# One root for all rows, ScalarE rounding for the recurrent gates, one PSUM pool through the up projection, and a new order of early weight loads, in a one-core decoder layer

## The chip, the cores and the metric

The kernel runs on one core of a Trainium2 chip. The metric is the device time of one execution in microseconds (us). All times below are counted from the start of the profiled span. TensorE is written PE in the profile, VectorE DVE, ScalarE ACT, GpSimd POOL and SyncE SP. SP and POOL issue DMAs here: SP plain ones, POOL those that add to what stands at the destination.

## What is computed

One layer on a sequence of 1024 rows of width 1024, in float32:

```
mod = c @ ada_w + ada_b                                  # six vectors: shift, scale, gate, twice
h   = rmsnorm(x) * g1 * (1 + sc1) + sh1
xr, yr, q, k, v, ga, gb = split(h @ w_in)                # seven "comps" of 1024 columns, numbered 0 to 6
xr  = causal_dwconv(xr)                                  # 4 taps
y_a = rg_lru(xr) * gelu(yr)                              # gates: sigmoid(xr @ wa), sigmoid(xr @ wx), per head of 128
y_b = stick_breaking_attention(rms(q), rms(k), v)        # 8 heads of 128
x   = x + gt1 * ((sigmoid(ga) * y_a + sigmoid(gb) * y_b) @ w_out)
h2  = rmsnorm(x) * g2 * (1 + sc2) + sh2
up  = causal_dwconv(h2 @ ffn_up)                         # 3 taps, 6144 columns: 24 pairs of gate and value blocks
out = x + gt2 * ((gelu(gate) * value) @ ffn_down)
```

## The kernel before

Every float32 product is made of three matmuls on rounded operands: each operand is split into a high part (rounded to fp32r) and a low part (the rest), and high times high, high times low and low times high are added up in PSUM. So each weight tile and each activation tile costs one cast (mostly ACT) and one subtraction (mostly DVE, `lo_of`).

**Opening** (about 0 to 76 us). Its order is written out by hand (`tc.manual_schedule()`), each engine's queue follows the program text. Eight tiles `xr` hold 128 rows of x each. `squares(t)` sums their squares on ACT, `norm(hf, on_act)` makes the reciprocal root (`rsqrt`, twelve small DVE instructions) for four rows at a time and scales these rows, some on ACT, the others on DVE. A unit n is a pair (j, hf): block j of 128 channels and half hf of the sequence. `channels(n)` transposes four 128x128 pieces on TensorE and lets ACT write the high part and a float32 copy, with shift and scale; `rest(n)` makes the low part on DVE. `scale_shift(j)` computes shift and scale of block j on DVE from two loaded tiles (`load_modulation`), each a dot product with the broadcast c. While units appear, three products of the first head are accumulated block by block: comps 3, 2 and 6 (`FIRST`). Their weights come with `first_load` and are split by `first_split` (cast on ACT, subtraction on POOL). The loop at the end of the opening runs over the sixteen units; turn n prepares unit n + 2 and multiplies unit n.

**Heads** (to 605 us): projections, attention and gate b of eight heads, in an order that a planner chooses from priorities and modelled costs.

**Recurrent stage** (605 to 865 us), planned too: for each head `lru_head` convolves on DVE and ACT, rounds the result `xc` to `xh` on POOL, subtracts `xl` on DVE and multiplies both with the gates' weights (L578 to L580); the activations follow on ACT, with changes of its table.

**Output projection** (to 945 us): `out_block(t)` for eight row blocks, accumulators `ao` from `acc_tile`, three buffers of two PSUM banks; evacuation on DVE (`og`). Half of the second normalization and of the up weights of steps 0 and 1 is prepared in between.

**Up projection** (945 to 1416 us), again by hand. It uses seven block products a step (Strassen's scheme on halves of channels and of the sequence), for 24 steps f. The sums of weight blocks are made by DMAs: a load on SP (`load`), then an accumulating DMA on POOL (`add`), and between the adds ACT and DVE split what stands there (`x1`, `x2_`, `x3`, `x4`). Six steps begin early (`early(f, n)`, twelve products on the first half of the sequence), interleaved by the slots `s_` of a list `plan` with `second_half(i)`, which normalizes the second half and reloads the first half from DRAM (`b11`, `b21` from `h2d`), and with `keep`, which splits the normalized sums. Each step needs accumulators bx and by (and bz where it didn't begin early), taken from `bank_tile`: after the output projection the PSUM pool is closed and a new pool `ups` gives six buffers of one bank.

**Down projection** (1416 us to the end): 24 blocks in four groups, its own PSUM pool.

## Time and profile before

| | |
|---|---|
| time, median of 3 runs | 1684.32 us (1684.28 to 1685.02) |
| the profiled execution's own time | 1682.83 us |
| its span in the profile | 1681.1 us |
| PE busy | 1634.8 us, 97% of the span |
| DVE, ACT, POOL busy | 1073.5, 798.4 and 219.9 us |
| bytes moved by DMA | 197.74 MB, mean 118 GB/s |

The span runs from the first to the last instruction of the core; the time of an execution is longer by what lies around it, here 1.7 us. A busy share is an average over all stages; what a stage waits for is in its own rows. The granted TensorE clock reads 1.00 in every stretch of the table of stages. Idle time of an engine counts only where TensorE, or whatever ends last, waits for it.

### The profile page before, as it was taken

The numbers are of one execution on the slowest core, as the hardware profiler recorded it, in microseconds if no ns is written. First come the engines' busy times: TensorE is split into PE (matmuls) and PEld (weight loads), VectorE is DVE, ScalarE is ACT, GpSimd is POOL, SyncE is SP. The second block draws the span as 40 slices with busy tenths as digits, with TensorE's granted clock in tenths as the row PEclk, the third lists the DMA queues.
The fourth block names the chain that finished last, engine by engine and source line by source line (L and its number), as shares of the span: only waits on it lengthen the run. The fifth ranks groups of instructions, "written<-read, shape, count | busy, mean of one in ns | idle before, by whom it ended". The sixth has DMA issues, their size and how long they took to land.

```text
span 1681.1 us, 22203 instructions
## 1 busy us (share of the span) xinstructions
PE 1634.8 (97%) x8170; PEld 1368.2 (81%) x8170; DVE 1073.5 (64%) x1739; ACT 798.4 (47%) x1338; POOL 219.9 (13%) x366
## 2 busy tenths in 40 slices
PE   3999999999999999989999999999999999999999
PEld 1898898898898887878888767888888887888887
DVE  6776857957857735856666568866666657425372
ACT  5645544644635526766464544444455445423100
POOL 2011111110100101310100122111111110001110
PEclk9999999999999999999999999999999999999999
DMA  8222322222222232221133597665566656514232
GB/s 316 88 76 78 99 76 76 85 86 82 76 86 85 76 125 70 72 79 57 44 124 145 203 229 184 150 147 134 128 140 143 147 119 201 175 63 151 67 121 100
DMA packets 94796, 197.74 MB, mean 118 GB/s; under 512 B 10128, under 2 KB 19552, under 8 KB 94688
## 3 DMA queue, kind: packets, MB, share of 16 engines
q1 hardware_dynamic: 80288, 170.11, 30.3%
q0 software_dynamic: 14400, 26.22, 9.5%
q8 instruction: 64, 1.05, 0.3%
q14 instruction: 44, 0.36, 0.1%
HBM read 164.79 MB, written 30.45 MB: 116 GB/s over the span
## 4 chain that ended last, share of the span: by engine, by line
PE 85%; DMA 4%; ACT 4%; DVE 4%; issue 2%; POOL 1%; SPq 0%; ACTq 0%; POOLq 0%; DVEq 0%
PE acc L150 27%; PE ad L1063 16%; PE bx L817 12%; PE by L817 6%; PE accv L393 6%; PE ao L662 5%; PE py L459 3%; PE bz L817 3%; PE tp L446 2%; DMA R<-in_ffn_up_dram 1%; DMA Q<-in_ffn_up_dram 1%; PE z L421 1%; PE z L422 1%; PE z L420 1%; ACT L550 1%
## 5 line engine op out<-in xcount | busy, mean ns | idle before, releaser
L769 POOL DMA_DIRECT2D R<-in_ffn_up_dram x72 | 63.4, 923 | 195.7 <-DVE ul L60 138.8
L1077 DVE TENSOR_TENSOR sum<-ad,sum 128x1024 f32<-128x1024 f32 (+1 forms) x26 | 29.4, 1140 | 85.6 <-PE ad L1063 84.0
L430 POOL TENSOR_SCALAR_AFFINE_SELECT stk<-stk 128x128 f32<-128x128 f32 x64 | 23.4, 366 | 409.0 <-ACT stk L425 392.0
L909 ACT COPY yv<-bx 128x512 f32<-128x512 f32 x36 | 21.2, 589 | 115.8 <-PE bx L817 115.8
L425 ACT ACTIVATE stk<-z,rkq 128x128 f32<-128x128 f32 (+3 forms) x96 | 57.2, 596 | 37.9 <-PE z L422 27.9
L574 POOL TENSOR_SCALAR xh<-xc 128x512 fp32r<-128x512 f32 x16 | 40.2, 2510 | 220.3 <-DVE xc L568 148.3
L60 DVE TENSOR_TENSOR ul<-Q,uh 128x512 fp32r<-128x512 f32 x42 | 28.9, 688 | 61.7 <-ACT uh L717 61.7
L60 DVE TENSOR_TENSOR ul<-R,uh 128x512 fp32r<-128x512 f32 x72 | 47.9, 687 | 31.2 <-ACT uh L717 31.2
L717 ACT CAST uh<-R 128x512 fp32r<-128x512 f32 x72 | 42.7, 618 | 51.8 <-DMA R<-in_ffn_up_dram 51.4
L438 DVE TENSOR_TENSOR_SCAN stk<-stk 128x128 f32<-128x128 f32 (+1 forms) x64 | 53.8, 841 | 15.5 <-POOL stk L434 9.9
L843 DVE SCALAR_TENSOR_TENSOR c<-yg,par,c 128x1023 f32<-128x1023 f32 (+1 forms) x48 | 61.5, 1280 | 2.8 <-ACT c L841 2.2
L843 DVE SCALAR_TENSOR_TENSOR c<-yv,par,c 128x1023 f32<-128x1023 f32 (+1 forms) x48 | 61.2, 1276 | 0.0
L135 DVE SCALAR_TENSOR_TENSOR ada<-ada,cb 128x1024 f32<-128x1024 f32 x48 | 60.4, 1271 | 0.0
L442 DVE TENSOR_TENSOR beta<-beta,stk 128x128 f32<-128x128 f32 (+3 forms) x96 | 54.0, 562 | 7.9
L60 DVE TENSOR_TENSOR al<-tp,ah 128x128 fp32r<-128x128 f32 (+3 forms) x96 | 51.7, 549 | 10.9 <-ACT ah L448 10.7
L448 ACT CAST ah<-tp 128x128 fp32r<-128x128 f32 (+3 forms) x96 | 45.4, 489 | 27.2 <-PE tp L446 19.1
L426 ACT ACTIVATE beta<-z,rkq 128x128 f32<-128x128 f32 (+3 forms) x96 | 57.0, 594 | 0.0
L446 PE MATMUL tp<-ident,beta 128*128 128x128 f32 x288 | 46.1, 274 | 0.0
L459 PE MATMUL py<-al,vh 128*128 128x256 f32 (+1 forms) x160 | 45.5, 284 | 0.0
L150 PE MATMUL acc<-hh,w_0h 128*128 128x512 f32 x96 | 37.6, 419 | 7.6 <-ACT w_0h L190 4.8
L459 PE MATMUL py<-ah,vl 128*128 128x256 f32 (+1 forms) x160 | 44.9, 281 | 0.0
L459 PE MATMUL py<-ah,vh 128*128 128x256 f32 (+1 forms) x160 | 44.2, 276 | 0.0
(522 smaller groups left out, 5496.4 us busy)
## 6 DMA issues: line engine op xcount, KB each, us to landing
ada<-in_ada_t_dram SPq DMA_DIRECT2D x48, 512.0 KB, 3.3
R<-in_ffn_up_dram POOLq DMA_DIRECT2D x72, 256.0 KB, 5.5
td<-c SPq DMA_DIRECT2D x24, 512.0 KB, 4.0
dn<-td SPq DMA_DIRECT2D x48, 256.0 KB, 7.0
dn<-in_ffn_down_dram SPq DMA_DIRECT2D x48, 256.0 KB, 3.4
R<-in_ffn_up_dram SPq DMA_DIRECT2D x24, 256.0 KB, 4.5
Q<-in_ffn_up_dram SPq DMA_DIRECT2D x24, 256.0 KB, 6.1
Q<-in_ffn_up_dram POOLq DMA_DIRECT2D x24, 256.0 KB, 4.0
```

Of the source, the lines that this page charges most:

```text
L60: return tt(out=out_, in0=full, in1=hi_.bitcast(F32), op=ALU.subtract)
L135: stt(out=t, in0=t, scalar=1.0, in1=cb, op0=ALU.mult, op1=ALU.mult, accum_out=mod[:, n:n + 1])
L150: mm(acc[hf], w[:, k % 4], r[k][hf], start=(k == 0 and i == 0), stop=(k == NB - 1 and i == 2))
L393: mm(acc[:, t * 2 * P:(t + 1) * 2 * P], r[k][hf][:, ts_], w[:, k % 2], start=(k == 0 and i == 0 and t == 0), stop=(k == NB - 1 and i == 2 ...
L425: act(st[:, :n], z[:, :n], AF.Sigmoid, scale=rkq[:, 16 + qb:17 + qb])
L446: nc.tensor.transpose(tp[:, t * P:(t + 1) * P], beta[:, t * P:(t + 1) * P], ident)
L459: mm(py[:, e0 * P:2 * P], vv[:, kb, d0:d0 + P], aa[kb // 4][:, kb % 4, e0:2], start=(kb == 0 and i == 0), stop=(kb == nkb - 1 and i == 2))
L662: mm(halves(acc, nf), m[k][hf][:, ts_], w[nf], start=(k == 0 and i == 0), stop=(k == NB - 1 and i == 2))
L769: nc.gpsimd.dma_start(blk(raw[f, key]), piece(f, row, half), accum_op=ALU.add)
L817: mm(bank, w[a][:, ks], Bm[n][b][k], start=(first and k == 0 and i == 0), stop=(last and k == 3 and i == 2), skip_group_check=True)
L843: stt(out=cs[f, i][:, d:], in0=y[:, :S - d], scalar=col("fw", (2 - d) * 48 + j), in1=cs[f, i][:, d:], op0=ALU.mult, op1=ALU.add)
L1063: mm(halves(acc, nf), dparts[f, hf][a][:, ts_], dparts[f, 2 + nf][w], start=(first and i == 0), stop=(last and i == 2))
```

## The change

Four edits, all in `trunk`.

1. Opening: the DMA queue begins with c and the modulation of block 0, then all eight rows of x, then the weights of comps 3 and 2, the modulation of block 1, the weights of comp 6 and the other modulations. One root is taken over all eight rows; two of the rows (3 and 4) are scaled on ACT, six on DVE. The subtraction for the low weights of the three first comps moves from POOL to DVE (`first_rest`). The first units' products are reordered: comp 3 of block 0 for both halves ahead of the loop, comps 2 and 6 of block 0 in the loop's first two turns.
2. Recurrent stage: `xh` is rounded by an ACT copy.
3. The PSUM pool of the output projection stays open through the up projection; `bank_tile` takes the first half of a buffer from `acc_tile` (three buffers of two banks), bz takes one of the two px banks.
4. Early loads of the up stage: the reloads of `b11` and `b21` stand one pair at a time between the early weights; `load_r(0)` comes third, `load_r(1)` and `load_r(2)` move into slots 2 and 8 of `plan`; `x1(0)` stands ahead of `keep(7, 2)` in slot 5.

```diff
--- before.py
+++ after.py
@@ -188,9 +188,12 @@
             wh = (W if htag == "wh" else m1).tile([P, 4, P], F32R, tag=htag, name=f"w{comp}_0h{i}", bufs=BUFS[htag])
             wl = (W if ltag == "wl" else m1).tile([P, 4, P], F32R, tag=ltag, name=f"w{comp}_0l{i}", bufs=BUFS[ltag])
             nc.scalar.copy(wh, raw)
-            nc.gpsimd.tensor_tensor(out=wl, in0=raw, in1=wh.bitcast(F32), op=ALU.subtract)
             parts.append((wh, wl))
         return parts
+
+    def first_rest(comp, raws):
+        for (wh, wl), raw in zip(first_w[comp], raws):
+            lo_of(wl, raw, wh)
 
 
 
@@ -199,16 +202,14 @@
     with tc.manual_schedule():
         xr = [btile(f"xr{t}") for t in range(NB)]
         raws, ada = {}, {}
-        for t in range(4):
+        nc.sync.dma_start(cb, c.broadcast_to((P, D)))
+        ada = {0: load_modulation(0)}
+        for t in range(NB):
             nc.sync.dma_start(xr[t], x[t * P:(t + 1) * P, :])
-        nc.sync.dma_start(cb, c.broadcast_to((P, D)))
-        raws[3] = first_load(3, "raw")
-        ada[0] = load_modulation(0)
-        for t in range(4, NB):
-            nc.sync.dma_start(xr[t], x[t * P:(t + 1) * P, :])
-        raws[2] = first_load(2, "pre")
+        raws = {3: first_load(3, "raw"), 2: first_load(2, "pre")}
+        ada[1] = load_modulation(1)
         raws[6] = first_load(6, "pre")
-        for j in range(1, 6):
+        for j in range(2, 6):
             ada[j] = load_modulation(j)
         first_w, hn = {}, {}
 
@@ -216,15 +217,18 @@
             junk = m1.tile([P, D], F32, tag="y", name=f"junk1_{t}", bufs=2)
             act(junk, xr[t], AF.Square, accum_out=ss[:, t:t + 1])
 
-        def norm(hf, on_act):
-
-            r = rsqrt(m1, ss[:, 4 * hf:4 * hf + 4], P, 4, 1.0 / D, f"r1_{hf}")
-            for t in range(4):
-                row = xr[4 * hf + t]
+        def weights(comp, htag, ltag):
+            first_w[comp] = first_split(comp, raws[comp], htag, ltag)
+            first_rest(comp, raws[comp])
+
+        def norm(on_act):
+
+            r = rsqrt(m1, ss, P, NB, 1.0 / D, "r1")
+            for t in range(NB):
                 if t in on_act:
-                    act(row, row, AF.Identity, scale=r[:, t:t + 1])
+                    act(xr[t], xr[t], AF.Identity, scale=r[:, t:t + 1])
                 else:
-                    tsc(out=row, in0=row, scalar1=r[:, t:t + 1], scalar2=None, op0=ALU.mult)
+                    tsc(out=xr[t], in0=xr[t], scalar1=r[:, t:t + 1], scalar2=None, op0=ALU.mult)
 
         def channels(n):
 
@@ -245,31 +249,26 @@
         units = [(j, hf) for j in range(NB) for hf in range(2)]
         first_acc = {comp: [pp.tile([P, H2], F32, tag=tag, name=f"acc{comp}_0_{hf}", bufs=2) for hf in range(2)]
                      for comp, tag in FIRST}
-        for t in range(4):
+        scale_shift(0, *ada.pop(0))
+        for t in range(NB):
             squares(t)
         first_w[3] = first_split(3, raws[3], "wh", "wl")
-        norm(0, (0, 2))
-        scale_shift(0, *ada.pop(0))
-        channels(0)
-        rest(0)
-        gemm(first_acc[3], first_w[3], hi, lo, (0,), (0,))
-        for t in range(4, NB):
-            squares(t)
-        first_w[2] = first_split(2, raws[2], "wh", "wl")
-        gemm(first_acc[2], first_w[2], hi, lo, (0,), (0,))
-        norm(1, (2,))
-        channels(1)
-        first_w[6] = first_split(6, raws[6], "beta", "sg")
-        gemm(first_acc[6], first_w[6], hi, lo, (0,), (0,))
-        rest(1)
+        norm((3, 4))
+        first_rest(3, raws[3])
+        for n in range(2):
+            channels(n)
+            rest(n)
+        weights(2, "wh", "wl")
+        for hf in range(2):
+            gemm(first_acc[3], first_w[3], hi, lo, (hf,), (0,))
         scale_shift(1, *ada.pop(1))
+        weights(6, "beta", "sg")
         for n, (j, hf) in enumerate(units):
             if n + 2 < len(units):
                 channels(n + 2)
                 rest(n + 2)
-            if n > 0:
-                for comp, _ in FIRST:
-                    gemm(first_acc[comp], first_w[comp], hi, lo, (hf,), (j,))
+            for comp, _ in FIRST[n < 2:]:
+                gemm(first_acc[comp], first_w[comp], hi, lo, (hf,), (j,))
             if n % 2 == 0 and n // 2 + 2 < NB:
                 scale_shift(n // 2 + 2, *ada.pop(n // 2 + 2))
             elif n // 2 + 6 < NB:
@@ -571,7 +570,7 @@
             rs, is_ = [], []
             for hf in range(2):
                 xh, xl = t2("xh", h, hf, F32R, 1), t2("xl", h, hf, F32R, 1)
-                nc.gpsimd.tensor_scalar(out=xh, in0=xcs[hf], scalar1=1.0, scalar2=None, op0=ALU.mult)
+                nc.scalar.copy(xh, xcs[hf])
                 lo_of(xl, xcs[hf], xh)
                 for i, (b, nm, lst) in enumerate((("ba", "r", rs), ("bx", "i", is_))):
                     pg = fps.tile([P, H2], F32, tag="px", name=f"pg{h}_{hf}_{b}", bufs=2)
@@ -674,6 +673,9 @@
 
             act(xt, xt, AF.Identity, scale=r2)
 
+        def bank_tile(name):
+            return halves(acc_tile(name), 0)
+
         def normed(hf, j, dsts):
 
             px = fps.tile([P, H2], F32, tag="px", name=f"px2{hf}_{j}", bufs=2)
@@ -745,16 +747,10 @@
                 parts_of(f, n, n)
         for t in range(4, NB):
             out_block(t)
-    banks.close()
 
 
     H = ctx.enter_context(tc.tile_pool(name="H", bufs=24, reuse_waits="tile"))
     F = ctx.enter_context(tc.tile_pool(name="F", bufs=1, reuse_waits="tile"))
-    fps = banks.enter_context(tc.tile_pool(name="ups", bufs=2, space=bass.MemoryType.PSUM, reuse_waits="tile"))
-
-    def bank_tile(name):
-        return fps.tile([P, H2], F32, tag="q", name=name, bufs=6)
-
     def htile(name, dt=F32R):
         return H.tile([P, H2], dt, tag="h", name=name)
 
@@ -915,7 +911,7 @@
             elif n == 6:
                 product(bx, f, 6, False, False)
             elif n == 2:
-                bz = bank_tile(f"bz{f}")
+                bz = fps.tile([P, H2], F32, tag="px", name=f"bz{f}", bufs=2)
                 product(bz, f, 2, True, True)
             elif n == 5:
                 product(bx, f, 5, False, False)
@@ -955,16 +951,27 @@
         split(full, Bm[n][0][i], Bm[n][1][i])
 
     with tc.high_priority(offset=AHEAD):
-        for q, key in enumerate(("Q", "Q", "a", "d", "d"), 4):
-            early_load(q // 2, q % 2 + 1, F.tile([P, H2], F32, tag=f"raw{key}", name=f"e{q}", bufs=RAWS[key]))
-            if q % 2:
-                for j in (q - 5, q - 4):
-                    nc.sync.dma_start(b11[j], h2d[j])
-                    nc.sync.dma_start(b21[j], h2d[4 + j])
-        for q in (9, 10):
-            early_load(q // 2, q % 2 + 1, w_raw(f"e{q}"))
-        for f in range(3):
-            load_r(f)
+        def load_b(*js):
+            for j in js:
+                nc.sync.dma_start(b11[j], h2d[j])
+                nc.sync.dma_start(b21[j], h2d[4 + j])
+
+        def early_raw(q, key):
+            t = F.tile([P, H2], F32, tag=f"raw{key}", name=f"e{q}", bufs=RAWS[key]) if key else w_raw(f"e{q}")
+            early_load(q // 2, q % 2 + 1, t)
+
+        early_raw(4, "Q")
+        early_raw(5, "Q")
+        load_r(0)
+        early_raw(6, "a")
+        load_b(0)
+        early_raw(7, "d")
+        load_b(1)
+        early_raw(8, "d")
+        load_b(2)
+        early_raw(9, None)
+        load_b(3)
+        early_raw(10, None)
 
     t3 = [None] * 4
 
@@ -986,11 +993,11 @@
             if q == 6:
                 early_load(5, 2, F.tile([P, H2], F32, tag="rawa", name="e11", bufs=RAWS["a"]))
 
-    plan = {3: [lambda: keep(7, 0, t3[0], htile), lambda: load_q(0)], 4: [lambda: keep(7, 1, t3[1], htile), lambda: load_yg(0)],
-            5: [lambda: keep(7, 2, t3[2], htile), lambda: x1(0), lambda: load_q(1)],
+    plan = {2: [lambda: load_r(1)], 3: [lambda: keep(7, 0, t3[0], htile), lambda: load_q(0)], 4: [lambda: keep(7, 1, t3[1], htile), lambda: load_yg(0)],
+            5: [lambda: x1(0), lambda: keep(7, 2, t3[2], htile), lambda: load_q(1)],
             6: [lambda: keep(7, 3, t3[3], htile), lambda: keep(6, 0, b11[0], atile), lambda: keep(6, 1, b11[1], atile)],
             7: [lambda: keep(6, 2, b11[2], atile), lambda: keep(6, 3, b11[3], atile), lambda: keep(5, 0, b12[0], atile)],
-            8: [lambda: keep(5, 1, b12[1], atile), lambda: x2_(0)],
+            8: [lambda: load_r(2), lambda: keep(5, 1, b12[1], atile), lambda: x2_(0)],
             9: [lambda: keep(5, 2, b12[2], atile), lambda: keep(5, 3, b12[3], atile), lambda: load_d(0), lambda: x1(1), lambda: load_yg(1)],
             10: [lambda: keep(3, 0, b22[0], htile), lambda: keep(3, 1, b22[1], htile), lambda: x3(0)],
             11: [lambda: keep(3, 2, b22[2], htile), lambda: keep(3, 3, b22[3], htile), lambda: keep(4, 0, b21[0], htile),
```

## Rows read from the trace of the kernel before

**Rows 1.** The table of stages of core 0: the stretch from the span's start and its length, then for TensorE (PE), its weight load, VectorE (DVE), ScalarE (ACT) and GpSimd (POOL) the busy time and in brackets the instructions, the granted TensorE clock, the share of the 16 DMA engines, GB/s.

```profile
0.00:20.00 20.00, 1.35 (x4) 0.58 (x4) 12.57 (x49) 9.87 (x16) 3.92 (x11) 1.00 0.92 341
20.00:40.00 20.00, 10.89 (x28) 6.27 (x29) 12.16 (x23) 10.59 (x18) 6.05 (x6) 1.00 0.80 297
...
605.00:865.00 260.00, 253.39 (x1109) 207.45 (x1110) 156.90 (x234) 157.97 (x234) 40.16 (x16) 1.00 0.20 65
...
950.00:975.00 25.00, 24.99 (x127) 20.60 (x126) 19.36 (x33) 17.93 (x31) 8.14 (x9) 1.00 1.05 323
...
1000.00:1050.00 50.00, 49.12 (x216) 39.98 (x214) 40.75 (x52) 20.80 (x27) 12.29 (x14) 1.00 0.83 191
1060.00:1400.00 340.00, 340.00 (x1502) 281.53 (x1501) 227.13 (x276) 165.44 (x249) 60.86 (x70) 1.00 0.60 137
```

**Rows 2.** What TensorE waited for over the whole span: its instruction, the one that released it, microseconds in total, how often, the longest.

```profile
PE pg_ba L578 <- POOL xh L574: 4.3, 3, 2.1
...
PE bx L817 <- ACT uh L717: 2.0, 2, 1.2
...
PE e L817 <- DVE og L666: 1.4, 1, 1.4
PE by L817 <- DVE ul L60: 1.3, 2, 0.7
PE bx L817 <- DVE yv L870: 1.1, 1, 1.1
...
PE pg_ba L579 <- DVE xl L60: 1.0, 1, 1.0
```

**Rows 3.** The table of stages again, for two stretches that begin with the span; the last column is the rate of the DMA engines.

```profile
0.00:11.50 11.50, 0.00 (x0) 0.00 (x0) 4.72 (x30) 6.30 (x11) 1.43 (x9) 1.00 0.83 286
0.00:18.00 18.00, 0.66 (x2) 0.29 (x2) 10.81 (x44) 9.68 (x15) 3.92 (x11) 1.00 0.91 335
```

**Rows 4.** The timeline of the opening, all engines: start, microseconds, engine, line, operation, tile written and tiles read, shapes, how many in a row, and in brackets the idle time before it with its releaser.

```profile
11.45 0.17 DVE L97 TENSOR_SCALAR r_0m<-ss 128x4 f32<-128x4 f32 x1 [2.93 <-ACT junk L217]
...
12.42 1.28 ACT L190 CAST w_0h<-w_0r 128x512 fp32r<-128x512 f32 x2 [1.00 <-DMA w_0r<-in_w_in_dram]
...
13.12 2.48 POOL L191 TENSOR_TENSOR w_0l<-w_0r,w_0h 128x512 fp32r<-128x512 f32 x2 [11.03 <-DMA w_0r<-in_w_in_dram]
13.24 1.16 DVE L102 SCALAR_TENSOR_TENSOR r_0t<-r_0r 128x4 f32<-128x4 f32 x1
14.44 1.18 DVE L103 TENSOR_TENSOR r_0t<-r_0t,r_0m 128x4 f32<-128x4 f32 x1
...
15.85 2.19 ACT L225 ACTIVATE xr<-xr,r_0r 128x1024 f32<-128x1024 f32 x2 [2.15 <-DVE r_0r L104]
15.85 1.42 DVE L227 TENSOR_SCALAR xr<-xr,r_0r 128x1024 f32<-128x1024 f32 x2
...
17.18 1.22 DVE L135 SCALAR_TENSOR_TENSOR ada<-ada,cb 128x1024 f32<-128x1024 f32 x1
...
19.61 0.15 DVE L174 TENSOR_TENSOR mod<-mod,par 128x1 f32<-128x1 f32 x1
...
20.68 0.80 PE L150 MATMUL acc<-hh,w_0h 128*128 128x512 f32 x1 [1.90 <-ACT hh L238]
...
39.52 0.78 ACT L238 ACTIVATE hh<-px,mod,s 128x512 fp32r<-128x512 f32 x1 [4.43 <-DVE mod L174]
...
41.02 0.66 PE L234 MATMUL px<-ident,xr 128*128 128x128 f32 x4 [0.22 <-ACT hn L238]
```

**Rows 5.** The chain that ended last, in order of time: start, microseconds, what. Two neighbouring groups of the opening's matmuls, and a DMA of the up stage.

```profile
62.87 2.08 PE acc L150 x9
65.38 2.08 PE acc L150 x9
...
972.38 10.23 DMA R<-in_ffn_up_dram
```

**Rows 6.** The instructions that touch the tile xh in the recurrent stage, its roundings: engine, operation, tiles, count, shortest, median and longest in ns, first and last start.

```profile
L574 POOL TENSOR_SCALAR xh<-xc x16: 1492/1768/5977, 620.3 to 842.0; 128x512 fp32r<-128x512 f32 x16
```

**Rows 7.** The timeline in the recurrent stage, columns as in rows 4.

```profile
730.00 1.28 ACT L550 ACT_TABLE_LOAD   x1
...
730.77 1.77 POOL L574 TENSOR_SCALAR xh<-xc 128x512 fp32r<-128x512 f32 x1 [20.63 <-DVE xc L568]
...
738.91 5.98 POOL L574 TENSOR_SCALAR xh<-xc 128x512 fp32r<-128x512 f32 x1 [6.37 <-DVE xc L568]
738.95 0.62 ACT L128 CAST w_5h<-w_5r 128x512 fp32r<-128x512 f32 x1
```

**Rows 8.** The timelines of ACT and of DVE at the opening of the up stage, columns as in rows 4.

```profile
969.62 0.63 ACT L717 CAST uh<-R 128x512 fp32r<-128x512 f32 x1 [1.84 <-DMA R<-in_ffn_up_dram]
...
982.69 0.62 ACT L717 CAST uh<-R 128x512 fp32r<-128x512 f32 x1 [6.80 <-DMA R<-in_ffn_up_dram]
...
995.49 1.14 ACT L717 CAST uh<-R 128x512 fp32r<-128x512 f32 x2 [5.39 <-DMA R<-in_ffn_up_dram]
...
971.33 0.69 DVE L60 TENSOR_TENSOR ul<-R,uh 128x512 fp32r<-128x512 f32 x1
```

**Rows 9.** The timeline in the middle of the up stage, columns as in rows 4.

```profile
1224.05 0.59 ACT L909 COPY yg<-bx 128x512 f32<-128x512 f32 x1 [1.10 <-PE bx L817]
...
1226.57 0.39 PE L817 MATMUL by<-b7h,uh 128*128 128x512 f32 x1
```

## Prediction

> **What bounds the kernel now.** I read the stages first, then the list of what TensorE waited for, then the timeline of each place that this list names. Over the whole span TensorE is busy 1634.8 of 1681.1 us, so a change can only pay by taking out some of the 46.3 us in which it idles, or lose by adding to them. By stage [rows 1]: it idles 18.65 us in the first 20 us and 9.1 in the next 20; 6.6 in the recurrent stage (605 to 865); none in 950 to 975, and none at all in the long up stage from 1060 to 1400. The waits [rows 2] say which edit can reach what: the rounding on POOL (xh) costs 4.3 us and the low part behind it (xl) 1.0; the evacuation of the last output block (og) costs the first early product 1.4; the waits for early and up weights (uh, ul, yv) are 2.0, 1.3 and 1.1, and one of 0.3 that I leave aside. So three places count: the opening, the recurrent stage, and the first 50 us of the up stage. Everywhere else TensorE is the bound and nothing in the diff takes matmuls away, so there the change is worth nothing unless it adds a wait.
>
> **Opening, bytes.** What must now land ahead of the last x row is par (161 KB), c, two modulation tiles and eight rows at 512 KB each: 5.93 MB. Before, 335 GB/s over the first 18 us moved 6.03 MB [rows 3], so these are through at about 17.7 us. Bytes and landing differ by a lag: the weights of comp 3 were 3.31 MB down the line, which 286 GB/s reach at 11.5 us, and ACT could cast them at 12.42 [rows 3, 4]. With that 0.9 us the last row is there at 18.6; its square takes 1.1 as the scaling of a row did, so the root starts at about 19.8. The modulation that heads the queue is dotted long before.
>
> **Opening, DVE and ACT.** The root of four rows took 4.4 us, 11.45 to 15.85, but two of its twelve instructions lasted 1.16 and 1.18 while POOL was subtracting weights (13.12, 2.48 us for two), and the others about 0.2 from start to start [rows 4]. The change takes POOL out of the opening, so I take 2.4 us for the root of eight: ready at 22.2. DVE scales six rows at 0.71 (rows 0 to 2 by 24.3, all by 26.5); the two on ACT take 2.2 and are earlier. Then in DVE's order: the low weights of comp 3, two at 0.69 (27.9; the price of a 128x512 subtraction on DVE [rows 8]), the low half of unit 0 (28.6), of unit 1 (29.3, its two ACT passes of 0.78 end about 28.6), the low weights of comp 2 (30.5 to 31), the second modulation, 17.18 to 19.76 before, thus 2.6 (33.1 to 33.7), the low weights of comp 6 (34.5 to 35). What is queued behind the root on DVE is all of this, and TensorE waits for each in turn: comp 3 starts at about 27 and not at 20.7; comp 2 follows at about 31; comp 6 has its first low weights at 34 and is through with both halves of block 0 at about 36. So the loop's third turn (transposes of block 2) starts at 36 to 38; I take 37. Before, it started at 41.02 [rows 4]. From there a turn costs TensorE 2.51 us [rows 5], two turns 5.0, while the chain modulation, two ACT passes and one subtraction is 2.6 + 1.56 + 0.69 = 4.85: TensorE stays the bound, and the lead is kept to the end of the stage. **Opening: -4.0 us.** Ends: -2.0 if the 15 or so matmuls ahead of that turn run no closer than twice the later 0.23 us (the lone first one lasted 0.80), or the rows land 2 us later; -5.5 if the turn starts with comp 6's weights at 35.5.
>
> **Recurrent stage.** Sixteen roundings leave POOL, 1.5 to 6.0 us each, median 1.77 [rows 6], 40.2 us in all, and become sixteen ACT copies; a cast of that shape on ACT took 0.62 (two in 1.28 [rows 4]). That adds 9.9 us to an ACT that is busy 158 of 260 us there [rows 1]; the idle 102 us cover it on average, but ACT is in order, so the place counts. The waits at xh are three, 4.3 us together, the longest 2.1 [rows 2]. That one stands behind the rounding of 730.77 to 732.54; ACT was loading a table until 731.28 [rows 7], so a copy behind this load is done at 731.9, 0.65 earlier. Another POOL rounding took 5.98 us from 738.91, and ACT was casting other weights at 738.95 for 0.62 [rows 7]: the copy is done by 740.2 there, nearly 5 us earlier. I take the other two waits, 2.2 us, as gone. The 1.0 at xl is a matter of DVE's order and stays. **Recurrent stage: -2.9 us.** Ends: -5.3 (4.3 at xh and 1.0 at xl) and +2: a copy that sits behind a table load and another cast (1.28 + 0.62 + 0.62 = 2.5 us against POOL's 1.8) in three heads where nothing covers it. The planner places the copy, so both are open.
>
> **Banks.** The first early product waited 1.4 us for og [rows 2] because the new pool's first bank lay under the last output block. With the old pool kept on, its bank is that of the block two before, long evacuated: the 1.4 goes there. In exchange the products rotate over three double banks, of which half is used, instead of six single ones, and a by may start only when the bx before it is evacuated. In the up stage that evacuation runs at 1224.05 for 0.59 and the next by starts at 1226.57 [rows 9]: 1.9 us to spare, and TensorE's own product 4, twelve matmuls at 0.23 [rows 5], 2.7 us, lies between, so I cost it at nothing; if that cover is gone, each of 23 steps pays what is missing. The Trainium skill (Perfetto Trace Analysis, Matmul Optimizations) wants all eight PSUM banks in use, which speaks against this edit; by it the sum would be that of the fourth case below, and only the spare 1.9 us of this trace stand against it. No run here shows three banks.
>
> **Early up weights.** The line ahead of the first product of step 0 is: weights R0 land, ACT casts (969.62, after 1.84 us of waiting for them), DVE subtracts (971.33), POOL issues an add that takes 10.23 us from 972.38, ACT casts again (982.69, after 6.80), and by the same pattern for step 1 at 995.49 after 5.39 [rows 5, 8]. The last of these ends last and sets TensorE's time from 996 on; whatever is won ahead of it, the 1.4 of the banks too, is lost there unless the line itself moves. R0 is now third in SP's order and not behind eight reloads, its cast stands ahead of a cast of B7 and not behind it: ACT does it 1.84 + 0.6 = 2.4 us sooner. DVE's half moves by 0.6 (only that place in its order) to 2.4; I take 2.0, since the work ahead of it also hangs on the early weights that now come before the reloads. Moved past: the load and add of R1 go behind the first reload's work, those of R2 to slot 8, on both SP's and POOL's queue. There the add of R2 stands ahead of the second adds of steps 0 and 1, which wait on POOL until R2 has landed. With the longest transfer of these rows, 10.2 us, an R2 issued near 973 is there by 983, and with a microsecond for each of the two adds ahead step 1's goes out at about 985 (an estimate). Before, it landed at 995.49, thus went out at about 985.3 if it took as long as step 0's: not later. The reloads of B11 and B21 come two or three places of 256 KB later, 2 us at 323 GB/s [rows 1]; what is made of them is first used after the twelve early products, which cover that. **Up opening, banks included: -2.0 us.** Ends: 0, and -6, all waits at og, uh, ul and yv. The Trainium skill (DMA: Bandwidth & Descriptors, Issuing engines are not separate DMA queues) says that SP's and POOL's transfers share the same 16 engines, so an order alone makes no room; the row of 950 to 975 with a DMA share of 1.05 [rows 1] agrees, and by the rule this term would be 0.
>
> **Sum.** -4.0 - 2.9 - 2.0 = -8.9 us. The profiled execution took 1682.8 us, so 1673.9 for one like it; it lay 1.5 under the median of the runs, 1684.3, so the median comes to 1675.4.
>
> **Rivals.** Second, only the opening pays: the ACT copies of xh wait behind table loads as long as POOL took, and the line of adds in the up opening is as long as before because the DMA engines are full. For it: share 1.05, and table loads of 1.28 us on ACT [rows 7]. Against it: ACT's idle 102 us, and R0's earlier place. 1684.3 - 4.0 = 1680.3. Third, the opening doesn't pay either: all of TensorE's work waits for eight rows and not four, and the third turn comes at 41 again. For it: the first matmul is 6 us later, and the DVE queue behind the root is long. Against it: before, TensorE stood still for 9 of the 20 us after its first matmul anyway. With the second case: no change, 1684.3; with the other gains intact 1679.4. Fourth, slower: three banks. Place: every step of the up stage; if the evacuation ends more than 2.7 us after product 3, by waits. It decides at 0.5 us a step: 24 x 0.5 = 12 eats the sum and more; at 0.8 us the time is 1675.4 + 19 = 1694. For it: early steps evacuate on DVE, which is 40.8 of 50 us busy there [rows 1]. Against it: the 1.9 us [rows 9].
>
> **How the numbers follow.** I give the forecast 0.50 (its own range 1671 to 1679), only the opening 0.25, no gain 0.15, slower 0.10. A measurement of this kernel can tell about 0.2%, 3.4 us. The second case lies at its edge on the faster side, so faster is 0.75, same 0.15, slower 0.10. The range takes the sum of the better ends down to 1668 and the second case and a part of the third up to 1683.
>
> **What would show it.** Right: first rows of the loop's third turn near 37 us; no POOL instruction between 605 and 865; no wait of TensorE at xh; the first early product directly behind the last output block; casts of R at about 967, 980 and 993; no wait of by for an ACT copy after 1060. Wrong: a root that starts after 21 us, or a third turn after 40; waits for the ACT copy of xh; TensorE resuming step 1 at 996 less the opening's and the recurrent stage's gains and no more; gaps of a constant size in every up step.

## The result, and the profile after

The changed kernel takes 1673.67 us (median of 4 runs, 1672.32 to 1675.29). Against the kernel before the ratio is 0.994, 95% interval 0.9922 to 0.9957: faster, by more than the 0.2% that a measurement of this kernel can tell. A second set of five runs on another chip gave 1672.98 us against 1683.62. The profiled execution took 1673.92 us, its span is 1672.2 us, 8.9 less than before.

The forecast was 1675.4 us, and its sum for the profiled execution, -8.9, is what the trace shows. Its parts are not: the opening gave 5.4 and not 4.0, the recurrent stage 3.5 and not 2.9, and the up opening nothing where 2.0 were forecast. That the sum was met is luck: two terms came out larger and made up for the one that did not come.

The table of stages of the changed kernel, columns and stretches as in [rows 1]:

```profile
20.00:40.00 20.00, 13.76 (x53) 9.88 (x54) 17.27 (x40) 13.26 (x20) 0.00 (x0) 1.00 1.02 380
...
605.00:865.00 260.00, 256.86 (x1128) 211.10 (x1128) 166.32 (x252) 172.51 (x261) 0.00 (x0) 1.00 0.21 67
...
950.00:975.00 25.00, 22.13 (x106) 18.24 (x105) 18.39 (x30) 14.19 (x26) 7.67 (x10) 1.00 0.99 274
...
1060.00:1400.00 340.00, 340.00 (x1502) 281.47 (x1500) 224.09 (x271) 166.99 (x251) 58.33 (x68) 1.00 0.60 141
```

What TensorE waited for, as in [rows 2]:

```profile
PE px L238 <- DVE xr L231: 24.8, 4, 24.2
PE bx L813 <- DVE es L825: 2.9, 1, 2.9
PE pg_ba L577 <- ACT xh L573: 2.5, 2, 1.9
PE bx L813 <- ACT uh L719: 2.3, 1, 2.3
```

In the recurrent stage TensorE idles 3.1 of 260 us and not 6.6, and POOL does nothing there any more. The steady up stage is full, as before. But between 950 and 975 there is now an idle of 2.9 us where there was none: the waits for og (1.4), ul (1.3) and DVE's yv (1.1) have left the list, and two longer ones, for es and for uh, stand in it.

The first matmuls of four stages show where the time went. These are rows by tile (line, engine, operation, tiles, count, shortest, median and longest in ns, first and last start) of the changed kernel: the first product of the heads, the output projection, the early products, the down projection.

```profile
L392 PE MATMUL accv<-wv0h,hh x64: 278/283/332, 71.2 to 96.2; 128*128 128x256 f32 x64
...
L661 PE MATMUL ao<-woh,mh x128: 387/389/496, 843.4 to 934.0; 128*128 128x512 f32 x128
...
L813 PE MATMUL e<-b1h,uh x24: 389/389/474, 935.1 to 968.3; 128*128 128x512 f32 x24
...
L1070 PE MATMUL ad<-d2h,d0h x96: 389/389/393, 1406.9 to 1634.0; 128*128 128x512 f32 x96
```

The same four of the kernel before:

```profile
L393 PE MATMUL accv<-wv0h,hh x64: 278/283/332, 76.6 to 101.6; 128*128 128x256 f32 x64
...
L662 PE MATMUL ao<-woh,mh x128: 387/389/501, 852.3 to 943.0; 128*128 128x512 f32 x128
...
L817 PE MATMUL e<-b1h,uh x24: 389/389/499, 945.6 to 979.0; 128*128 128x512 f32 x24
...
L1063 PE MATMUL ad<-d2h,d0h x96: 389/389/389, 1415.8 to 1642.9; 128*128 128x512 f32 x96
```

The lead is 5.4 us after the opening, 8.9 at the output projection, 10.5 at the early products (the og wait is gone), and 8.9 again at the down projection: 1.6 us were won and given back inside the up opening.

Single traces differ by about 1 us. In the nine traces of this document with the new opening as a whole the heads begin at 70.0 to 71.2 us (the trace above is the latest of them), in the four with the old one at 76.2 to 77.2: the opening is worth about 6.3 us in the mean. From there to the output projection it is 772.0 to 773.2 us in the ten traces with the rounding on ACT and 775.4 to 776.0 in the four with it on POOL, about 3.1 in the mean.

### The profile page after: what moved, and what is told of

Read it like the earlier page. It is cut to its first block, busy times and chain, and to the rows that moved or that the text cites. A ratio compares the mean times of both kernels' runs of the same rounds, so it can differ in the third digit from the quotient of the medians.

```text
span 1672.2 us, 22174 instructions
## 1 busy us (share of the span) xinstructions
PE 1631.8 (98%) x8170; PEld 1371.2 (82%) x8170; DVE 1068.2 (64%) x1734; ACT 806.0 (48%) x1353; POOL 170.3 (10%) x344
## 5 line engine op out<-in xcount | busy, mean ns | idle before, releaser
L813 PE MATMUL bx<-b6h,uh 128*128 128x512 f32 x96 | 38.7, 403 | 5.2 <-DVE es L825 2.9
```

Source lines behind the costliest of these rows:

```text
L813: mm(bank, w[a][:, ks], Bm[n][b][k], start=(first and k == 0 and i == 0), stop=(last and k == 3 and i == 2), skip_group_check=True)
```

## Experiments: each edit alone

Four kernels make one edit each in the kernel before. All were timed on one chip, where before took 1682.87 us.

**The opening alone** (all hunks up to the loop over units):

```diff
-        for t in range(4):
-            squares(t)
...
+        norm((3, 4))
+        first_rest(3, raws[3])
```

> The kernel before with the opening of the change alone. Theory, from the two traces: the third turn of the loop starts at 36.7 us and not at 41.0, the loop then runs without the three small waits that it had before, the heads begin 5.4 us earlier, and since TensorE is the bound from there to the recurrent stage, the whole time falls by 5.4 us (ratio 0.9968). Prediction's term: 4.0 us. Rival: part of the 5.4 us comes from the rounding on ACT, which let the planner order the opening's end otherwise; then the heads begin only 4 us earlier here.

Measured: 1676.88 us, ratio 0.9964 (0.9952 to 0.9976), -6.0. The heads begin at 70.4.

**The rounding on ACT alone:**

```diff
-                nc.gpsimd.tensor_scalar(out=xh, in0=xcs[hf], scalar1=1.0, scalar2=None, op0=ALU.mult)
+                nc.scalar.copy(xh, xcs[hf])
```

> The kernel before with only the rounding of xh moved from POOL to ACT. Theory: the waits of TensorE at xh and xl fall from 5.3 us to about 2.5, and with the pipeline restarts saved the time falls by 3 to 3.5 us (ratio 0.998). Rival: the recurrent stage owes its gain to its earlier start or to the planner's order after the other edits; then this kernel keeps 4 us or more of waits and its time is that of before.

Measured: 1678.04 us, 0.9969 (0.9957 to 0.9981), -4.8. The output projection starts at 849.5, 2.8 us sooner. The waits at xh are still three, together 3.1 us; the one at xl is gone. The down projection starts at 1410.4, 5.4 us sooner, so 2.6 more came in the up stage, with nothing changed there. About 2 of them can be placed: TensorE waits 0.45 us for step 1's uh and not 1.23, and the waits for low halves at 1019 and 1047 of the kernel before are gone. Why those weights came sooner was not settled.

**The banks alone:**

```diff
+        def bank_tile(name):
+            return halves(acc_tile(name), 0)
-    banks.close()
-    fps = banks.enter_context(tc.tile_pool(name="ups", ...))
-                bz = bank_tile(f"bz{f}")
+                bz = fps.tile([P, H2], F32, tag="px", name=f"bz{f}", bufs=2)
```

> The kernel before with only the PSUM pool kept open through the up projection. Theory: the first early product follows the last output block 1.4 us sooner, but step 1's first weights come by the same line of adds as before, so from 996 us on nothing has moved: 0 us, and the products of step 0 wait longer in between. Rival: the 1.4 us stay to the end (ratio 0.9992). Second rival: three rotating buffers cost something in every one of 24 steps, 5 us or more slower.

Measured: 1682.71 us, 1.0002 (0.9993 to 1.0011): no difference. The first early product starts 1.6 us sooner, and from 980 on the first waits of TensorE become these (timeline of TensorE, only the rows with an idle time):

```profile
984.89 0.47 PE L814 MATMUL bx<-b6h,uh 128*128 128x512 f32 x1 [2.39 <-DVE es L826]
...
992.02 0.50 PE L814 MATMUL bx<-b5h,uh 128*128 128x512 f32 x1 [1.05 <-DVE yv L867]
...
996.49 0.50 PE L814 MATMUL bx<-b6h,uh 128*128 128x512 f32 x1 [1.42 <-ACT uh L720]
```

But the 1.4 us of og are lost ahead of that, at 957.57. There transposes wait as long for an evacuation on ACT, which itself stands (956.75) behind a cast that waited 2.60 us for its early weights; in the list of waits, columns as in [rows 2]:

```profile
PE px L684 <- ACT n L686: 1.4, 1, 1.4
```

The last matmul of the early products before step 0 starts at 982.11, in the kernel before at 982.18, and step 1 at 996.49, before at 996.15. That the line would have taken the 1.4 us by itself, as expected, is not shown here. In this execution, the fastest of eleven, the down projection still starts 1.4 us sooner (1414.4); the median shows nothing of it.

**The new order of loads alone** (the last two hunks of the diff):

```diff
-            if q % 2:
-                for j in (q - 5, q - 4):
-                    nc.sync.dma_start(b11[j], h2d[j])
...
+        early_raw(5, "Q")
+        load_r(0)
+        early_raw(6, "a")
+        load_b(0)
```

> The kernel before with only the new order of early up weights, reloads and adds. Theory: the cast of R0 comes 2 to 2.6 us sooner, but R0's second add goes out on POOL no sooner than before, because R1's add now stands ahead of it there and waits for R1 to land; so step 1's first weights are cast within 0.7 us of 995.5 and the time is that of before. Rival, the prediction's term: the line is 2 us shorter and the time falls by 2 us (ratio 0.9988).

Measured: 1686.18 us, 1.0018 (1.0009 to 1.0026): 3.3 us slower. In its profiled execution (1.8 above its median) TensorE waits 3.85 us for uh ahead of step 1, and the granted clock reads 0.50 from 997.8 to 1004.6:

```profile
998.62 0.80 PE L817 MATMUL bx<-b6h,uh 128*128 128x512 f32 x1 [3.85 <-ACT uh L717]
```

R1's second add leaves when it did before (986.62, before 986.79), but the cast behind it comes at 997.95, not within 0.7 us of 995.5 as expected; what made that transfer longer was not settled. So the edit from which I had taken most of the last term costs time when it is made alone. The four differences add up to -7.7 us; the whole change gave -10.6 against the same-chip runs of before in the second set.

## Experiments: parts undone in the changed kernel

**The first weights' low parts back on POOL** (one run, not repeated):

```diff
-            lo_of(wl, raw, wh)
+            nc.gpsimd.tensor_tensor(out=wl, in0=raw, in1=wh.bitcast(F32), op=ALU.subtract)
```

> The changed kernel with the three subtractions of first weights back on POOL. Theory (DVE instructions with two inputs stand while POOL subtracts): the twelve instructions of the root take 4 us or more and not 2.4, the rows are scaled 2 us later, and what DVE saves later, three pairs of 1.29 us, gives about that back, so the third turn starts between 36 and 39 us. Rival (the root of before was slow for another reason): the root takes 2.4 us and the third turn starts at 35 us or sooner.

Measured: 1676.86 us in one run; the heads begin at 75.1 and not at 71.2. VectorE's timeline shows the root, and below it the POOL instruction beside it:

```profile
19.99 0.17 DVE L97 TENSOR_SCALAR r1m<-ss 128x8 f32<-128x8 f32 x1 [7.79 <-ACT junk L218]
...
20.61 1.23 DVE L102 SCALAR_TENSOR_TENSOR r1t<-r1y 128x8 f32<-128x8 f32 x1
21.86 1.19 DVE L103 TENSOR_TENSOR r1t<-r1t,r1m 128x8 f32<-128x8 f32 x1
23.09 0.17 DVE L104 SCALAR_TENSOR_TENSOR r1r<-r1t,r1y 128x8 f32<-128x8 f32 x1
...
24.49 4.07 DVE L231 TENSOR_SCALAR xr<-xr,r1r 128x1024 f32<-128x1024 f32 x6
```

```profile
20.54 2.49 POOL L196 TENSOR_TENSOR w_0l<-w_0r,w_0h 128x512 fp32r<-128x512 f32 x2 [18.44 <-ACT w_0h L190]
```

The root takes 4.5 us again (19.99 to 24.49), and exactly the two instructions that meet POOL's subtraction last 1.23 and 1.19. That the root of four rows was slow because of POOL was read from [rows 4]; here it is shown, on a root of eight. The third turn begins at 40.53, later than both theories had it: POOL takes 6.95 us for the four subtractions of comps 2 and 6 (from 31.15), and TensorE waits 2.01 us for one of them. So by this one trace the move of these subtractions to VectorE carries most of the opening's gain: without it the heads begin only 1.5 us sooner than in the kernel before.

**Six banks again** (the pool of the kernel before, with everything else changed):

```diff
-            return halves(acc_tile(name), 0)
+            return fps.tile([P, H2], F32, tag="q", name=name, bufs=6)
```

> The changed kernel with the six single banks of the kernel before in a pool of their own. Theory: the first early product waits 1.4 us again for the last output block, the first product of step 0 starts about 1.4 us sooner than in the changed kernel since it no longer waits for an evacuation on DVE, but step 1's weights set the time, so the end is within 0.5 us of the changed kernel. Rival: three banks cost something in the steps that follow; then this is faster by 1 us or more.

Measured: 1675.90 us, 0.9957 (0.9944 to 0.9971). The og wait of 1.4 is back, the es wait is gone, and step 1 waits 3.81 us for uh. Three banks are no slower; the intervals of the two kernels overlap, so that they are faster isn't shown.

## Experiments: the line of adds

In the changed kernel the last cast of the line, R1's at 986.53, still ends last. POOL's timeline says why (DMA issues; R0's first add, R1's, Q0's, R0's second, then R2's with R0's third, R1's second):

```profile
945.13 1.03 POOL L765 DMA_DIRECT2D R<-in_ffn_up_dram  x1 [367.43 <-DVE ul L60]
...
958.43 0.86 POOL L765 DMA_DIRECT2D R<-in_ffn_up_dram  x1 [7.97 <-PE e L813]
...
960.39 0.85 POOL L765 DMA_DIRECT2D Q<-in_ffn_up_dram  x1 [0.23 <-DMA yg<-yed]
...
962.02 1.89 POOL L765 DMA_DIRECT2D R<-in_ffn_up_dram  x1
...
973.92 1.73 POOL L765 DMA_DIRECT2D R<-in_ffn_up_dram  x2 [9.12 <-DMA R<-in_ffn_up_dram]
976.74 0.85 POOL L765 DMA_DIRECT2D R<-in_ffn_up_dram  x1 [1.08 <-DVE ul L60]
```

and ACT's, where these tiles are cast:

```profile
956.45 0.61 ACT L719 CAST uh<-R 128x512 fp32r<-128x512 f32 x1
...
972.64 0.62 ACT L719 CAST uh<-R 128x512 fp32r<-128x512 f32 x1 [7.79 <-DMA R<-in_ffn_up_dram]
...
986.53 1.14 ACT L719 CAST uh<-R 128x512 fp32r<-128x512 f32 x2 [6.48 <-DMA R<-in_ffn_up_dram]
```

Counted from the first early product, R0's cast comes 2.6 us sooner than before (21.4 us, against 24.0), DVE's half of it 1.2 sooner (24.5, 25.7), and R0's second add not at all (27.0, 26.7). VectorE takes 1.4 us back:

```profile
957.51 0.69 DVE L983 TENSOR_TENSOR t<-n,n 128x512 f32<-128x512 f32 x1
...
959.57 0.68 DVE L60 TENSOR_TENSOR ul<-R,uh 128x512 fp32r<-128x512 f32 x1
```

Three subtractions of `second_half`, from 957.51 on, stand ahead of R0's. POOL takes the rest: it stood until 958.43 in front of R1's add, whose load was issued at 948.86 only, and what had piled up behind (Q0's add, three adds of `second_half`) had to leave before R0's, which goes 1.8 us after DVE is done; before, it went after 0.4. The releaser named for R1's add is a product long done; with this add moved (below), it leaves at about the same time, and the row names its own transfer.

**R1's add behind R0's second** (slot 5), and the same with R0's first split in slot 4:

```diff
-    plan = {2: [lambda: load_r(1)], 3:
+    plan = {2: [lambda: load(1, "R", 1, 0)], 3:
-            5: [lambda: x1(0), lambda: keep(7, 2, t3[2], htile),
+            5: [lambda: x1(0), lambda: add(1, "R", 1, 1), lambda: keep(7, 2, t3[2], htile),
...
# the second kernel, with slot 2 as above:
+    4: [lambda: x1(0), lambda: add(1, "R", 1, 1), lambda: keep(7, 1, t3[1], htile), lambda: load_yg(0)],
+    5: [lambda: keep(7, 2, t3[2], htile), lambda: load_q(1)],
```

> The changed kernel with one move: R1's accumulating add goes from slot 2 to slot 5, behind R0's second add, its load stays in slot 2. Theory (POOL's queue holds the line up): the adds of the reloads and of Q0 no longer stand behind R1's landing, R0's second add goes out about 1.7 us sooner against the first early product, the cast behind it and step 1's weights too, and TensorE's waits at bx, 5.2 us in the changed kernel, fall by 1 to 2 us. Rival (the DMA engines are full, so an add lands when the bytes ahead of it are through): the add goes out sooner and lands at the same time, waits and time as in the changed kernel.

> The changed kernel with step 0's first split (x1 of 0) and R1's add moved to slot 4, R1's load still in slot 2. Theory: R0 is there by 953 or so, so its cast and subtraction come about 3 us sooner, R0's second add leaves 4 to 5 us sooner, the weights behind it are there before the twelve early products end, the wait of 2.9 us at bx goes, that of 2.3 us shrinks or goes, and the clock doesn't fall after them: 3 to 7 us faster than the changed kernel. Rival (DMA engines full): not over 2.5 us, which is what they stood idle between 971 and 975 us.

Measured: 1672.77 (0.9945, 0.9933 to 0.9958) and 1677.39 us (0.9962, 0.9949 to 0.9975). Neither is faster than the changed kernel beyond the intervals. POOL's timeline of the second kernel:

```profile
961.85 0.84 POOL L765 DMA_DIRECT2D Q<-in_ffn_up_dram  x1 [8.26 <-DMA yed<-es]
...
962.92 2.40 POOL L765 DMA_DIRECT2D R<-in_ffn_up_dram  x2
```

With R1's add out of the way, Q0's is next in line and waits 8.26 us (for its own load, as the next kernel's row says; here the row names another transfer). R0's second add goes out behind it, at 962.92, 9.6 us after its tile was cast at 953.36.

**R1's and Q0's adds behind R0's second:** as the second kernel, and in slot 3 only Q0's load:

```diff
-    3: [lambda: keep(7, 0, t3[0], htile), lambda: load_q(0)],
+    3: [lambda: keep(7, 0, t3[0], htile), lambda: load(0, "Q", 0, 0)],
+    4: [lambda: x1(0), lambda: add(1, "R", 1, 1), lambda: add(0, "Q", 1, 0), ...
```

> The changed kernel with the first split of R0 in slot 4 and, on POOL, R0's second add directly behind its first, with R1's add and Q0's add (both of which stood ahead of it) now behind it. Theory (POOL's order is what holds the line): in the two runs that moved only R1's add, POOL's next wait was that for Q0's load, and R0's second add left 119.9 to 120.3 us after the first output block; here it leaves at about 112, is cast at about 121 and not 129, and the last cast of the line (step 1) comes at about 136 and not 143. The waits of TensorE at bx for uh and es (2.9 + 2.3 us in the changed kernel) go, the granted clock stays at 1.00, the down projection starts some 6 us sooner than in the changed kernel (1401), and the time is about 1668 us (1666 to 1670). Rival (the DMA engines are full, share above 1 from 948 to 971, so no order makes room): R0's second add leaves earlier but lands within 2 us of where it did, the step-1 cast stays at 142 to 145, and the time is 1673 to 1677.

Measured: 1673.94 us, 0.9943 (0.9931 to 0.9956); the changed kernel beside it on this chip 1672.98, 0.994 (0.9928 to 0.9953).

> The changed kernel itself on the chip of a_adds, for the comparison with it: every theory expects 1673 to 1675 us, ratio 0.994.

Neither theory held as it stood. Counted from the first output block, R0's second add leaves at 113.3 us (after: 118.6), its cast follows at 122.7 (129.2), and step 0 runs without a wait. R1 is cast at 124.6. But its second add leaves only with the three of the last row (the first two are R1's and Q0's, now behind R0's):

```profile
957.78 0.84 POOL L765 DMA_DIRECT2D R<-in_ffn_up_dram  x1 [0.94 <-DMA R<-in_ffn_up_dram]
962.37 0.85 POOL L765 DMA_DIRECT2D Q<-in_ffn_up_dram  x1 [3.75 <-DMA Q<-in_ffn_up_dram]
...
972.75 2.60 POOL L765 DMA_DIRECT2D R<-in_ffn_up_dram  x3 [2.83 <-DMA R<-in_ffn_up_dram]
```

The first of the three at 972.75 is R2's, which waited for R2's load; R0's third and R1's second stand behind it. The cast for step 1 comes at 142.1 (after: 143.1), TensorE waits 6.44 us for it, and the granted clock falls afterwards. The engines were not too full to bring R0 sooner; the next add in POOL's order took the block over.

**And Q1's load out of the full stretch** (from slot 5 to slot 9):

```diff
-            5: [lambda: keep(7, 2, t3[2], htile), lambda: load_q(1)],
+            5: [lambda: keep(7, 2, t3[2], htile)],
+            9: [..., lambda: x1(1), lambda: load_yg(1), lambda: load_q(1)],
```

> As a_adds, and the load and add of Q1 (256 KB each) move from slot 5 to slot 9, out of the full stretch. Theory (POOL's order alone): no further gain, the time within 2 us of a_adds, or worse where Q1 comes late for product 7 of step 1. Rival (bytes): 0.52 MB less ahead of R0's adds at 323 GB/s is 1.6 us, so the step-1 cast comes 1.5 us sooner than in a_adds and the time is 1 to 2 us lower.

Measured: 1672.34 us, 0.9936 (0.9922 to 0.9950), 1.6 less than without it, step 1's cast at 140.3 and not 142.1. The earlier cast is what the bytes theory expected, one trace against one; the intervals of the two times overlap, so a gain in time is not shown, and the time fits both theories.

**And R2's add behind R1's second:**

```diff
-            8: [lambda: load_r(2), lambda: keep(5, 1, b12[1], atile), lambda: x2_(0)],
+            8: [lambda: load(2, "R", 1, 0), lambda: keep(5, 1, b12[1], atile), lambda: x2_(0)],
+            9: [..., lambda: x1(1), lambda: add(2, "R", 1, 1), lambda: load_yg(1), lambda: load_q(1)],
```

> As a_adds_q1, and R2's add moves on POOL from ahead of the second adds of steps 0 and 1 to behind step 1's. In a_adds_q1 POOL waits 9.3 us for R2's load and then issues three adds in 2.6 us, the last of them step 1's, while ACT had cast that tile at 124.0 us after the first output block. Theory (POOL's order): step 1's add now leaves at about 127 and not 130.5, its cast comes at 137 to 138 and not 140.3, TensorE's wait at bx for uh falls from 4.3 to about 1.5 us, the granted clock keeps or loses less, the down projection starts 3 to 4 us sooner (1401 to 1403), and the time is about 1669 us (1667.5 to 1670.5). Rival (full DMA engines, share 1.06 up to 980): the transfer takes the longer, the cast stays at 140 to 142, and the time is 1671.5 to 1674.

Measured: 1668.83 us (1666.73 to 1669.94), 0.9916 (0.9903 to 0.9930): 14.5 us under the 1683.34 of before on its chip, and 4 to 5 under the medians of the changed kernel on other chips. The stage itself shows it: from the first output block to the down projection it is 557.0 us, in the two traces of the changed kernel 563.5 and 562.6. R0's third add, R1's second and R2's:

```profile
967.45 0.86 POOL L765 DMA_DIRECT2D R<-in_ffn_up_dram  x1 [4.33 <-DVE ul L60]
969.85 0.85 POOL L765 DMA_DIRECT2D R<-in_ffn_up_dram  x1 [1.54 <-DVE ul L60]
972.21 0.86 POOL L765 DMA_DIRECT2D R<-in_ffn_up_dram  x1 [1.51 <-DMA R<-in_ffn_up_dram]
```

Each leaves when its data is ready. Step 1's cast comes at 136.1:

```profile
978.67 1.14 ACT L719 CAST uh<-R 128x512 fp32r<-128x512 f32 x2 [5.01 <-DMA R<-in_ffn_up_dram]
```

TensorE waits 0.16 us for it, and the down projection starts at 1399.6, 7.3 us sooner than in the changed kernel's first trace; 0.8 of this was there at the output projection already (842.6). The clock shows in the stages of the changed kernel, first, and of this one (columns as in [rows 1]):

```profile
971.00:974.00 3.00, 0.85 (x4) 0.38 (x2) 0.71 (x2) 1.36 (x3) 0.08 (x1) 1.00 0.65 156
975.00:979.00 4.00, 4.00 (x12) 3.09 (x11) 4.00 (x8) 4.00 (x9) 1.50 (x2) 0.57 0.91 244
...
988.90:992.40 3.50, 3.50 (x10) 2.67 (x10) 1.50 (x4) 0.33 (x1) 1.03 (x2) 0.51 0.85 155
```

```profile
971.00:974.00 3.00, 3.00 (x15) 2.49 (x14) 3.00 (x6) 2.66 (x6) 0.86 (x1) 1.00 1.08 296
975.00:979.00 4.00, 4.00 (x19) 3.14 (x17) 1.23 (x3) 0.33 (x1) 0.00 (x0) 1.00 1.09 286
...
988.90:992.40 3.50, 3.50 (x17) 2.92 (x16) 0.30 (x1) 0.95 (x2) 0.00 (x0) 1.00 1.11 234
```

The other 6.5 us can be counted: in the changed kernel two waits, 2.87 and 2.33 us, and behind each about eight matmuls 0.43 us apart instead of 0.23, 1.6 us each time, 8.4 together; here waits at by and bx of 0.9 and 0.2 remain, and one of 0.8 for yv at the first product of the down projection is new.

## Where the prediction was right and where it failed

**Opening: the mechanism was right, the size short, by 1.4 us in the first trace and 2.3 in the mean of nine.** Of the changed kernel, ACT's last square, VectorE's root and the first scaling, and TensorE's third turn (three timelines):

```profile
19.75 1.06 ACT L218 ACTIVATE junk<-xr 128x1024 f32<-128x1024 f32 x1 [0.18 <-DMA xr<-in_x_dram]
```

```profile
20.93 0.17 DVE L97 TENSOR_SCALAR r1m<-ss 128x8 f32<-128x8 f32 x1 [7.82 <-ACT junk L218]
...
23.35 4.07 DVE L231 TENSOR_SCALAR xr<-xr,r1r 128x1024 f32<-128x1024 f32 x6
```

```profile
36.69 0.60 PE L238 MATMUL px<-ident,xr 128*128 128x128 f32 x4
```

The last row landed 1.1 us later than the byte count said (19.7, not 18.6), the root took the 2.4 us forecast, and the third turn began at 36.69 where I took 37. That is 4.3 us under [rows 4]. The other 1.1 us is what I had not looked for: I assumed that the loop of the kernel before ran at 2.51 us a turn from its third turn on. Its transposes stand at 41.02, 43.70, 46.80 and later 59.37 and 62.27, so three turns took 2.68, 3.10 and 2.90, waiting for low halves among others (0.30 us at 44.84). After the change all turns take 2.5, and the lead at the last transposes is 5.5 (64.33 against 69.81). The third rival, that eight rows would cost as much as they bring, fell.

**Recurrent stage: right, 0.6 short in the first trace, 0.2 in the mean.** The roundings are now the following row, 0.62 us as taken from [rows 4], and POOL is idle there.

```profile
L573 ACT CAST xh<-xc x16: 607/615/622, 615.3 to 831.1; 128x512 fp32r<-128x512 f32 x16
```

The waits at xh are two of 1.9 and 0.6 us (4.3 in three before), and the 1.0 at xl, which I left standing, is gone. The two roundings that I read, ahead of the products at 732.60 and 744.94 in the kernel before, hold nothing up any more, where I had left 1.4 us of the first; the 1.9 stands where 0.5 stood before (663.28, now 659.26), and the 0.6 is new. So 2.8 us of waits went, close to the 2.9 forecast, but the term was right in sum more than in its places.

**Up opening: the step that failed.** I priced the line by R0's first cast (2.4 us sooner) and DVE's half of it (2.0). The cast came 2.6 sooner, DVE's half 1.2, inside the bounds I gave it. Then I let the gain pass through POOL, although I had written that R1's load and add move behind the first reload: I gave that place no price, and POOL spent what was left. R2's add, which I did name and priced as "not later", was not the block in the changed kernel, but it was the next one but one: it decided in the run that moved the two others away. (R1's second add left at 986.79 in the kernel before, not at the 985.3 that I had estimated from its landing.) And I had no term for the clock: 3.2 of the 8.4 us that the two new waits cost here are slow matmuls behind them. The forecast sign of failure was exact: TensorE resumes step 1 at 987.20, 8.95 us before the 996.15 of the kernel before, which is the opening and the recurrent stage and no more. The casts that I forecast at 967, 980 and 993 were told in the time of before; 8.9 us earlier they would be 958, 971 and 984, and they came at 956.45, 972.64 and 986.53. The gain runs out along the line.

By the rule of the Trainium skill that I weighed (DMA: Bandwidth & Descriptors, Issuing engines are not separate DMA queues) this term would be 0, and 0 it was. But the reason was another: the last run, whose DMA share still reads 1.06 to 1.08 from 965 to 980 (0.89 in the mean in the changed kernel), gained by a new order of the same transfers. The engines are shared; what was late was the issue.

**Banks: right in the steady stage, wrong in the first step.** The og wait went, and no step between 1060 and 1400 waits; the one of 0.7 us at 1401.00 stood in the kernel before too (1409.65). That the rotation costs nothing I had argued from [rows 9], a steady step, where ACT evacuates. In the first step the bank is freed by VectorE, in order behind a subtraction that waits for the line:

```profile
973.29 0.69 DVE L60 TENSOR_TENSOR ul<-R,uh 128x512 fp32r<-128x512 f32 x1 [6.41 <-ACT uh L719]
973.89 0.68 DVE L825 TENSOR_TENSOR es<-e,es 128x512 f32<-128x512 f32 x1
```

TensorE waits 2.87 us for this es. With the line repaired (the last run) the wait isn't there, with three banks still: it was the line's wait, reached through DVE's order. The fourth rival, 0.5 us a step, did not come. The Trainium skill's advice to use all eight banks (Perfetto Trace Analysis, Matmul Optimizations) would have that rival win; these runs show three rotating buffers no slower than six.

**The median** came 1.7 us lower than forecast although the sum was met: I had added 1.5 us because the profiled run of before lay that much under its median, while the changed kernel's lay at its own.

## What to carry to other kernels

When a transfer is moved, follow every instruction that it brings to the queues of both its engines, and ask of each what it waits for: an add that waits for its load holds up all adds behind it, however early their own data is there. Issue such adds in the order in which their data will be ready, and move all blocks at once, since each one taken away alone uncovers the next and shows no gain. Check a buffer rotation in its first turns, where other engines free the buffers, and not only in the steady stage.

## What the runs showed of the hardware

A wait of TensorE can cost more than its length. After idle times of 2.87 and 2.33 us in the changed kernel the granted clock fell from 1.00 to 0.5 (the lower of its levels, 1.2 GHz) for about 3.4 us each time, and around the wait of 3.85 us in the run with the loads alone it read 0.50 for 6.8. But idle times of 2.39 us with the banks alone, 3.10 in the second trace of the changed kernel and 3.63 with R1's add in slot 5 left it at 1.00, while in that second trace it fell to 0.51 behind a wait of 1.87. So the length of the wait alone does not say whether it falls, and these rows do not show what does.

The first matmuls of the opening started mostly 0.4 to 0.8 us apart in both kernels, until about 33 us after the change and 39 before, where later ones start 0.23 apart, though the granted clock reads 1.00 in these stretches; what holds them there these runs don't show.
